# Rows for all 128 partitions: transfers with a repeated source and a matmul with ones in place of GpSimd's partition_broadcast

## The chip, the core and the metric

The kernel runs on one core of one Trainium2 chip. A core has a matrix engine (TensorE, PE in the profile, with its weight loads shown apart as PEld), a vector engine (VectorE, DVE), a scalar engine (ScalarE, ACT), GpSimd (POOL), and SyncE (SP), which here issues nearly all transfers between HBM and the on-chip memory. Each engine works through its own queue in the order that was fixed when the program was built, and waits where an operand isn't there yet. The metric is the device time of one execution in microseconds (us). PE's granted clock is given as a share of 2.4 GHz: 1.00 is 2.4 GHz, 0.50 is 1.2 GHz.

## What is computed

One decoder layer on x of 512 tokens by 1024 features, in float32. Three blocks follow one another, each with a normalization ahead (a gain row of 1024 numbers) and one behind (another gain row), so there are six gain rows in all:

```python
h = rms_norm(x, ffn1_pre_g)
x = x + 0.5 * rms_norm(swiglu(h, ffn1_w_gate, ffn1_w_up, ffn1_w_down), ffn1_post_g)
h = rms_norm(x, mix_pre_g)
proj = h @ w_in
...
mixed = jnp.concatenate([attn, ssm], axis=-1) @ w_out
x = x + rms_norm(mixed, mix_post_g)
h = rms_norm(x, ffn2_pre_g)
x = x + 0.5 * rms_norm(swiglu(h, ffn2_w_gate, ffn2_w_up, ffn2_w_down), ffn2_post_g)
```

`rms_norm(x, g)` is x times 1/sqrt(mean(x*x) + eps) times g, row by row. The mixer needs, beside matrices, three rows of 16 numbers (dt_bias, a_log, d_skip) and one number lambda, which is an exponential of two dot products.

## The kernel before

**Tiles.** Tokens lie on the 128 partitions, so x is four tiles t = 0 to 3 of 128x1024, and a gain row that multiplies a tile must stand in every partition: a tile of 128x1024 floats, 512 KB. `bcast` (L128 to L134) makes one: a 4 KB transfer into a tile `row` of one partition, and then `partition_broadcast` on GpSimd into the tile `t`. The three rows of 16 and lambda are put into one row of 49 numbers and go the same way, at L118, into `prm`. Both take their tiles from pools with few buffers (`ka` has 3).

**Normalization ahead of a block.** `prenorm_T` (L150) handles one tile. ACT squares and sums it (L147), POOL turns the sum into 1/sqrt(...) in two small operations (`rstd`, L140 and L141, tile `r`), DVE multiplies the tile by `r` and by the gain (L156, tile `kb`), PE transposes the result in eight pieces of 128x128 (L160), and ACT and DVE evacuate that in a high and a low part (L163), because every product is made of three passes over such split operands (`mm3`, L194 to L196).

**Start.** The program loads x tile 0, the gain `ffn1_pre_g`, x tile 1, and then the weights of the first four products of the FFN (two gate and two up blocks of 128 columns, `lead` in `ffn`, four 512 KB transfers named `raw`). Each weight is split on ACT (L175, `whi`) and on DVE (L177, `wlo`). Tiles 0 and 1 are normalized first, and the four lead products run on the token columns 0 to 255 (lines L228 and L194 to L196). x tiles 2 and 3 are loaded behind the lead weights, are normalized by `rest1`, with their transposes set into the last lead product, and then the lead products run on the columns 256 to 511. Further gain rows are fetched by `gain(...)`: for the first block while the lead products run. The rest of an FFN is a long stretch of products.

**Middle.** The mixer runs attention (`attention`, with lines L554 to L598), projections, and the chunked scan (`ssd`), woven into each other by fixed ratios. At the head of a chunk of the scan, `decay` has POOL make two 128x1024 products of a mask and a column (L641, tiles `kb` from `u` and `ah`, then from `u` and `al`), PE multiplies them (L653), and ACT takes the exponential (L654).

**Second FFN.** Built as the first: `rest2` (L913) normalizes tiles 2 and 3 while the lead products run on the first half.

**Order.** The build schedules the queues by a simulation of the engines, so a row in the code does not tell its place in a queue. On POOL the build puts a row named ISA ahead of each `partition_broadcast`, and another ahead of the next ordinary operation; in the trace these show as MODIFY_POOL_CONFIG, and are called a switch here. The broadcast itself is also printed as ISA.

Of the kernel before, what the change touches and what calls it, by code (L numbers as in the profile page):

```python
# [17 lines left out]
P = 128  # L18
D = 1024
# [10 lines left out]
class Layer:  # L30
# [48 lines left out]
    def mixer_consts(s, conv_w, conv_b, dt_bias, a_log, d_skip, subln, norm_g, lq1, lk1, lq2, lk2):  # L79
        nc = s.nc  # L80
        s.ones = s.t([P, P], F32, "ones")
        nc.gpsimd.memset(s.ones, 1.0)
        s.u1 = s.t([P, P], F32, "u1")
        nc.gpsimd.affine_select(s.u1, s.ones, pattern=[[-1, P]], base=-1, channel_multiplier=1,
                                compare_op=ALU.is_ge, fill=0.0)
        s.u2 = s.t([P, P], F32, "u2")
        nc.gpsimd.affine_select(s.u2, s.ones, pattern=[[1, P]], base=0, channel_multiplier=-1,
                                compare_op=ALU.is_ge, fill=0.0)

        rows = s.m((P, P))  # L90
        nr = 61 + 8
        nc.sync.dma_start(rows[0:48, :], conv_w.rearrange("k (t p) -> (k t) p", p=P))
        nc.sync.dma_start(rows[48:60, :], conv_b.rearrange("o (t p) -> (o t) p", p=P))
        nc.sync.dma_start(rows[60:61, 0:64], subln)
        nc.sync.dma_start(rows[60:61, 64:128], subln)
        nc.sync.dma_start(rows[61:69, :], norm_g.rearrange("o (t p) -> (o t) p", p=P))
        ps = s.pb()
        nc.tensor.transpose(ps[:, :nr], rows[:nr, :], s.ident[:nr, :nr])
        s.cols = s.t([P, nr], F32, "cols")
        nc.vector.tensor_scalar_mul(s.cols, ps[:, :nr], 0.5)  # L100
        nc.vector.tensor_scalar_mul(s.cols[:, 60:61], ps[:, 60:61], 1.0 - LAMBDA_INIT)

        row = s.m((1, 48 + 128))
        nc.sync.dma_start(row[:, 0:16], dt_bias)
        nc.sync.dma_start(row[:, 16:32], a_log)
        nc.sync.dma_start(row[:, 32:48], d_skip)
        for i, l in enumerate((lq1, lq2, lk1, lk2)):
            nc.sync.dma_start(row[:, 48 + 32 * i:80 + 32 * i], l)
        lam = s.t([1, 4], F32, "lam")
        nc.vector.tensor_mul(row[:, 48:112], row[:, 48:112], row[:, 112:176])  # L110
        nc.vector.tensor_reduce(lam[:, 0:2], row[:, 48:112].rearrange("p (a b) -> p a b", a=2),
                                axis=AX.X, op=ALU.add)
        nc.scalar.activation(lam[:, 0:2], lam[:, 0:2], AF.Exp)
        nc.scalar.activation(row[:, 16:32], row[:, 16:32], AF.Exp)
        nc.vector.tensor_scalar(row[:, 48:49], lam[:, 1:2], lam[:, 0:1], -LAMBDA_INIT,
                                op0=ALU.subtract, op1=ALU.add)
        s.prm = s.t([P, 49], F32, "prm")
        nc.gpsimd.partition_broadcast(s.prm, row[:, 0:49])  # L118
        s.nlam = s.prm[:, 48:49]

        s.qscale = s.t([P, 4], F32, "qscale")
        s.nslope = s.t([P, 48], F32, "nslope")[:, :16]
        for h in range(8):
            lo = (h % 2) * 64
            nc.gpsimd.memset(s.qscale[lo:lo + 64, h // 2:h // 2 + 1], 32.0 ** -0.5 * 2.0 ** (h + 1))
            nc.gpsimd.memset(s.nslope[:, 2 * h:2 * h + 2], -2.0 ** -(h + 1))

    def bcast(s, ap):  # L128
        nc = s.nc
        row = s.k4([1, D])  # L130
        nc.sync.dma_start(row, ap)
        t = s.k4([P, D])
        nc.gpsimd.partition_broadcast(t, row)
        return t  # L134


# [822 lines left out]
```

## Time and profile before

| what | us |
|---|---|
| median of 3 runs (1141.47 to 1144.44) | 1143.95 |
| the profiled execution, its own time | 1141.0 |
| its span, from the first to the last instruction | 1138.9 |
| mean granted PE clock in it | 0.981 |

The profile is of one execution. A time given for an instruction or a wait is from that execution, counted from the start of its span. In the timeline a row gives start, duration, engine, line, operation, tiles written and read, and in brackets how long the engine was idle before it and what ended that. "issue" there means that the engine waited for nothing that the profile can see. The table of windows gives busy time of each engine in a stretch, the granted PE clock, the mean share of the 16 DMA engines and what they moved.

### The profile page before, as it was taken

The page shows a single profiled execution, that of the slowest core. Times are in us where ns is not written, and L with a number is a line of the kernel's source. Part 1 is how long each engine was busy: PE and PEld are TensorE (multiplying, and loading weights), DVE is VectorE, ACT ScalarE, POOL GpSimd, SP SyncE. Part 2 cuts the span into 40 slices and gives each one's busy share as a digit, 9 for nine tenths or more (in the row PEclk, how much of TensorE's full clock was granted, in tenths as well). Part 3 has the DMA queues.
Part 4 walks back from the last instruction along what each step waited for, and adds up shares of the span by engine and source line. Part 5 has one row for each costly group of instructions (what it writes and reads, how often), then busy time and mean ns, then how long its engine had stood idle before and what let it go on. Part 6 is the DMA issues. An engine that isn't in the chain of part 4 may idle for free. (4 is left out here: it accounts for less than half of the span.)

```text
span 1138.9 us, 13158 instructions
## 1 busy us (share of the span) xinstructions
PE 1072.2 (94%) x5129; PEld 893.3 (78%) x5129; DVE 547.6 (48%) x861; ACT 396.9 (35%) x673; POOL 89.5 (8%) x123
## 2 busy tenths in 40 slices
PE   2699999999999999999997989986999999999997
PEld 2688888888888887888875777876888888888885
DVE  2333433434333663686875987663234343353334
ACT  3242121322322453465652445443322212132231
POOL 3100000000000210000113351020000000000001
PEclk9899999999999999999998999997999999999999
DMA  5143241433323244543321103231333224143311
GB/s 166 56 128 94 70 133 56 130 93 107 97 93 95 93 126 138 156 128 104 93 75 38 56 19 110 76 111 56 106 98 93 93 73 131 56 130 97 106 38 74
DMA packets 135444, 107.94 MB, mean 95 GB/s; under 512 B 5772, under 2 KB 116432, under 8 KB 135382
## 3 DMA queue, kind: packets, MB, share of 16 engines
q1 hardware_dynamic: 134806, 105.00, 30.7%
q0 software_dynamic: 576, 2.10, 0.5%
q8 instruction: 40, 0.66, 0.2%
q14 instruction: 22, 0.18, 0.0%
HBM read 96.60 MB, written 4.19 MB: 88 GB/s over the span
## 5 line engine op out<-in xcount | busy, mean ns | idle before, releaser
L175 ACT CAST whi<-raw 128x1024 fp32r<-128x1024 f32 x176 | 183.2, 1051 | 496.0 <-PE pa L195 210.9
L195 PE MATMUL pa<-blk,whi 128*128 128x512 f32 (+1 forms) x864 | 332.4, 385 | 0.0
L196 PE MATMUL pa<-blk,wlo 128*128 128x512 f32 (+1 forms) x864 | 331.0, 385 | 0.0
L177 DVE TENSOR_TENSOR wlo<-raw,whi 128x1024 fp32r<-128x1024 f32 x176 | 217.6, 1244 | 230.8 <-ACT whi L175 225.1
L194 PE MATMUL pa<-blk,whi 128*128 128x512 f32 (+1 forms) x736 | 279.3, 380 | 0.0
L196 PEld LDWEIGHTS pa<-blk,wlo 128*128 128x128 f32 x864 | 163.3, 189 | 32.7 <-issue 1.2
L195 PEld LDWEIGHTS pa<-blk,whi 128*128 128x128 f32 x864 | 163.4, 189 | 31.7 <-issue 0.7
L194 PEld LDWEIGHTS pa<-blk,whi 128*128 128x128 f32 x736 | 138.3, 188 | 26.3
L258 DVE TENSOR_TENSOR at<-cv,pa 128x512 f32<-128x512 f32 x42 | 28.9, 687 | 130.4 <-PE pa L196 130.4
L195 PE MATMUL pa<-wlo,blk 128*128 128x512 f32 x216 | 85.3, 396 | 0.0
L196 PE MATMUL pa<-whi,blk 128*128 128x512 f32 x216 | 84.8, 396 | 0.0
L140 POOL TENSOR_SCALAR r<-ss 128x1 f32<-128x1 f32 x32 | 12.9, 405 | 805.7 <-DVE ss L332 728.9
L283 PE MATMUL pb<-whi,blk 128*128 128x512 f32 x224 | 65.1, 389 | 0.0
L192 PE MATMUL pa<-blk,whi 128*128 128x512 f32 x128 | 52.8, 412 | 0.0
L283 PEld LDWEIGHTS pb<-whi,blk 128*128 128x128 f32 x224 | 41.9, 188 | 8.6
L194 PE MATMUL pa<-whi,blk 128*128 128x512 f32 x120 | 47.3, 394 | 0.0
L196 PEld LDWEIGHTS pa<-whi,blk 128*128 128x128 f32 x216 | 40.3, 188 | 8.6 <-issue 0.5
L195 PEld LDWEIGHTS pa<-wlo,blk 128*128 128x128 f32 x216 | 40.7, 188 | 8.1 <-issue 0.7
L290 DVE TENSOR_TENSOR blk<-blk,pb 128x512 f32<-128x512 f32 x24 | 15.4, 683 | 64.3 <-PE pb L283 64.3
L160 PE MATMUL pt<-ident,kb 128*128 128x128 f32 x72 | 11.7, 309 | 32.6 <-DVE kb L156 31.5
L283 PE MATMUL po<-whi,blk 128*128 128x512 f32 x112 | 41.3, 389 | 0.0
L283 PE MATMUL pa<-whi,blk 128*128 128x512 f32 x112 | 41.3, 389 | 0.0
(207 smaller groups left out, 1394.6 us busy)
## 6 DMA issues: line engine op xcount, KB each, us to landing
raw<-in_ffn_w_gate_dram SPq DMA_DIRECT2D x44, 512.0 KB
raw<-in_ffn_w_up_dram SPq DMA_DIRECT2D x44, 512.0 KB
raw<-in_ffn_w_down_dram SPq DMA_DIRECT2D x44, 512.0 KB
raw<-in_w_in_dram SPq DMA_DIRECT2D x32, 512.0 KB
blk<-kc SPq DMA_DIRECT2D x96, 64.0 KB
raw<-in_w_out_dram SPq DMA_DIRECT2D x12, 512.0 KB
blk<-in_x_dram SPq DMA_DIRECT2D x4, 512.0 KB
x_d<-blk POOLq DMA_DIRECT2D x4, 512.0 KB, 3.5
```

What stands on the lines that cost most here:

```text
L140: nc.gpsimd.tensor_scalar(r, ss, mul / n, eps, op0=ALU.mult, op1=ALU.add)
L160: ins = nc.tensor.transpose(ps[:, i * P:(i + 1) * P], hx[:, (4 * b + i) * P:(4 * b + i + 1) * P], s.ident)
L175: s.nc.scalar.copy(hi, raw)
L177: s.nc.vector.tensor_sub(lo, raw, hi)
L192: mm(ps, a[0], b[0], start=first, stop=False)
L194: mm(ps, a[0], b[0], start=first, stop=False)
L195: mm(ps, a[0], b[1], start=False, stop=False)
L196: return mm(ps, a[1], b[0], start=False, stop=last).ins
L258: nc.vector.tensor_mul(pr, sg, pu)
L283: nc.tensor.matmul(pd[c], a[:, ts], w[:, c * S:(c + 1) * S], start=st, stop=sp)
L290: nc.vector.tensor_add(a, a, pd[c])
```

## The change

`bcast` no longer has a row tile and a GpSimd operation: one transfer fills all 128 partitions, with the same 4 KB of HBM as the source of each. `prm` is made by a matmul of a row of 128 ones with the row of 49, into a PSUM buffer of the tag `pb`, and a copy on DVE.

```diff
         s.prm = s.t([P, 49], F32, "prm")
-        nc.gpsimd.partition_broadcast(s.prm, row[:, 0:49])
+        ps = s.pb()
+        nc.tensor.matmul(ps[:, 0:49], s.ones[0:1, :], row[:, 0:49], start=True, stop=True)
+        nc.vector.tensor_copy(s.prm, ps[:, 0:49])
         s.nlam = s.prm[:, 48:49]
...
     def bcast(s, ap):
         nc = s.nc
-        row = s.k4([1, D])
-        nc.sync.dma_start(row, ap)
         t = s.k4([P, D])
-        nc.gpsimd.partition_broadcast(t, row)
+        nc.sync.dma_start(t, ap.broadcast_to([P, D]))
         return t
```

The queues follow. SP issues the transfers of the start; `blk` are the x tiles, `ka` the gain tiles, `raw` the weights. Before:

```order
L768 DMA blk_70<-in_x_dram 128x1024
L131 DMA ka_73<-in_ffn_pre_g_dram 1x1024
L768 DMA blk_70<-in_x_dram 128x1024
L185 DMA raw_131<-in_ffn_w_gate_dram 128x8x128
L185 DMA raw_162<-in_ffn_w_up_dram 128x8x128
L185 DMA raw_195<-in_ffn_w_gate_dram 128x8x128
L185 DMA raw_226<-in_ffn_w_up_dram 128x8x128
L131 DMA ka_2264<-in_ffn_post_g_dram 1x1024
L768 DMA blk_71<-in_x_dram 128x1024 x2
L272 DMA raw_410<-in_ffn_w_down_dram 128x1024
L131 DMA ka_2268<-in_mix_pre_g_dram 1x1024
```

And with the change:

```order
L768 DMA blk_70<-in_x_dram 128x1024
L133 DMA ka_73<-in_ffn_pre_g_dram 128x1024
L768 DMA blk_70<-in_x_dram 128x1024
L185 DMA raw_129<-in_ffn_w_gate_dram 128x8x128
L185 DMA raw_160<-in_ffn_w_up_dram 128x8x128
L185 DMA raw_193<-in_ffn_w_gate_dram 128x8x128
L185 DMA raw_224<-in_ffn_w_up_dram 128x8x128
L133 DMA ka_2262<-in_ffn_post_g_dram 128x1024
L133 DMA ka_2264<-in_mix_pre_g_dram 128x1024
L768 DMA blk_71<-in_x_dram 128x1024 x2
L272 DMA raw_408<-in_ffn_w_down_dram 128x1024
```

The gain transfers are 128 rows instead of one, and that of `mix_pre_g` now stands ahead of x tiles 2 and 3 instead of behind them.

On POOL, at the start, between the making of the identity matrix and the first two normalizations, before:

```order
masks.py:199 AFFINE_SELECT ident_63<-ident_63 128x128
L133 ISA
L133 ISA ka_75<-ka_73 128x1024
L140 ISA
L140 TENSOR_SCALAR r_85<-ss_83 128x1
L141 TENSOR_TENSOR r_85<-r_85,mhalf_68 128x1
```

And with the change:

```order
masks.py:199 AFFINE_SELECT ident_63<-ident_63 128x128
L140 TENSOR_SCALAR r_83<-ss_81 128x1
L141 TENSOR_TENSOR r_83<-r_83,mhalf_68 128x1
L140 TENSOR_SCALAR r_106<-ss_104 128x1
L141 TENSOR_TENSOR r_106<-r_106,mhalf_68 128x1
```

The broadcast and the two switches around it are gone from the queue; nothing takes their place.

On POOL, at the head of the scan's chunks in the middle, before:

```order
L641 TENSOR_TENSOR kb_4545<-u_424_2676,ah_3145 128x1024
L133 ISA
L133 ISA ka_5591<-ka_5589 128x1024
L641 ISA
L641 TENSOR_TENSOR kb_4547<-u_424_2676,al_3146 128x1024
L641 TENSOR_TENSOR kb_4563<-u_424_2676,ah_3145 128x1024
L133 ISA
L133 ISA ka_5595<-ka_5593 128x1024
L641 ISA
L641 TENSOR_TENSOR kb_4565<-u_424_2676,al_3146 128x1024
```

And with the change:

```order
L598 TENSOR_TENSOR ms_750_4200<-ms_750_4200,mhalf_68 128x8
L641 TENSOR_TENSOR kb_4541<-u_421_2670,ah_3141 128x1024
L641 TENSOR_TENSOR kb_4543<-u_421_2670,al_3142 128x1024
L641 TENSOR_TENSOR kb_4559<-u_421_2670,ah_3141 128x1024
L641 TENSOR_TENSOR kb_4561<-u_421_2670,al_3142 128x1024
L641 TENSOR_TENSOR kb_4677<-u_421_2670,ah_3141 128x1024
L598 TENSOR_TENSOR ms_806_4441<-ms_806_4441,mhalf_68 128x8
L641 TENSOR_TENSOR kb_4679<-u_421_2670,al_3142 128x1024
```

Two broadcasts with four switches stood between the two halves of a chunk's products; the halves now follow one another. The other places on POOL are alike: seven broadcasts and their 14 switches are gone. PE has one row more, the matmul for `prm`, and DVE one, its copy.

## Rows read from the trace of the kernel before

**Rows 1.** Page, section 1: busy us (share of the span) xinstructions

```profile
PE 1072.2 (94%) x5129; PEld 893.3 (78%) x5129; DVE 547.6 (48%) x861; ACT 396.9 (35%) x673; POOL 89.5 (8%) x123
```

**Rows 2.** Waits of PE: who waited for whom: us, times, longest

```profile
PE pt L160 <- DVE kb L156: 31.5, 2, 21.5
PE pb L160 <- DVE kb L156: 12.2, 1, 12.2
PE pb L653 <- POOL kb L641: 10.1, 2, 8.0
PE pb L696 <- DVE kc L678: 1.8, 1, 1.8
```

**Rows 3.** Timeline of POOL: the broadcasts and the operations behind them

```profile
10.52 1.30 POOL L133 PARTITION_BROADCAST ka<-ka  x1 [8.89 <-issue]
19.79 0.18 POOL L140 TENSOR_SCALAR r<-ss 128x1 f32<-128x1 f32 x1 [7.97 <-issue]
42.62 0.18 POOL L140 TENSOR_SCALAR r<-ss 128x1 f32<-128x1 f32 x1 [8.24 <-issue]
588.17 1.89 POOL L641 TENSOR_TENSOR kb<-u,al 128x1024 fp32r<-128x1024 f32 x1 [7.02 <-issue]
607.83 1.89 POOL L641 TENSOR_TENSOR kb<-u,al 128x1024 fp32r<-128x1024 f32 x1 [7.39 <-issue]
776.32 0.18 POOL L140 TENSOR_SCALAR r<-ss 128x1 f32<-128x1 f32 x1 [7.65 <-issue]
```

**Rows 4.** Windows: length; busy us of PE, PEld, DVE, ACT, POOL; PE clock; DMA; GB/s

```profile
2.00:15.00 13.00, 0.00 (x0) 0.00 (x0) 0.00 (x0) 3.41 (x6) 1.30 (x1) 1.00 0.97 317
44.90:48.40 3.50, 3.45 (x17) 3.48 (x18) 2.58 (x3) 1.18 (x2) 0.55 (x1) 0.50 0.02 5
560.00:580.00 20.00, 20.00 (x102) 16.87 (x102) 19.27 (x45) 10.98 (x28) 3.73 (x3) 1.00 0.27 70
588.00:620.00 32.00, 21.87 (x93) 17.97 (x94) 16.34 (x22) 9.23 (x15) 10.52 (x6) 0.79 0.10 34
591.00:594.50 3.50, 3.50 (x10) 2.75 (x9) 1.89 (x3) 1.54 (x3) 1.90 (x1) 0.51 0.42 150
609.80:615.00 5.20, 5.20 (x12) 4.12 (x13) 2.61 (x4) 1.75 (x3) 3.55 (x2) 0.50 0.01 3
778.50:782.10 3.60, 3.54 (x17) 3.54 (x18) 2.58 (x5) 2.10 (x3) 0.00 (x0) 0.50 0.00 0
```

**Rows 5.** Timeline of ACT: start, first work on each of three transfers

```profile
4.37 1.06 ACT L147 ACTIVATE kb<-blk 128x1024 f32<-128x1024 f32 x1 [2.30 <-DMA blk<-in_x_dram]
6.71 1.06 ACT L147 ACTIVATE kb<-blk 128x1024 f32<-128x1024 f32 x1 [1.18 <-DMA blk<-in_x_dram]
8.54 1.04 ACT L175 CAST whi<-raw 128x1024 fp32r<-128x1024 f32 x1 [0.69 <-DMA raw<-in_ffn_w_gate_dram]
```

**Rows 6.** Timelines of the engines: a normalization, from sum to products

```profile
410.38 1.06 ACT L147 ACTIVATE kb<-blk 128x1024 f32<-128x1024 f32 x1 [4.28 <-DVE blk L336]
...
411.90 0.56 POOL L141 TENSOR_TENSOR r<-r,mhalf 128x1 f32<-128x1 f32 x1
...
22.55 1.41 DVE L156 SCALAR_TENSOR_TENSOR kb<-blk,r,ka 128x512 f32<-128x512 f32 x2 [0.45 <-POOL r L141]
...
25.14 1.25 PE L228 MATMUL pa<-blk,whi 128*128 128x256 f32 x8 [0.17 <-ACT blk L163]
...
44.95 1.94 PE L160 MATMUL pt<-ident,kb 128*128 128x128 f32 x8 [10.03 <-DVE kb L156]
```

**Rows 7.** Timelines of ACT and PE, second FFN, tiles 2 and 3

```profile
762.12 1.06 ACT L147 ACTIVATE kb<-blk 128x1024 f32<-128x1024 f32 x1 [3.34 <-DVE blk L336]
...
765.37 1.03 PE L160 MATMUL pt<-ident,kb 128*128 128x128 f32 x8
```

**Rows 8.** Timelines of PE and DVE: a small matmul, the row of 49

```profile
412.66 0.22 PE L98 MATMUL pb<-ident,m 69*128 69x69 f32 x1
...
416.81 0.20 DVE L115 TENSOR_SCALAR m<-lam 1x1 f32<-1x1 f32 x1 [0.27 <-ACT lam L113]
```

## The prediction

> **What bounds the kernel now.** I read the page first: PE is busy for 1072.2 of 1138.9 us [rows 1]. The kernel is bound by its products, and a change that touches none of them can win only PE's 67 idle us and what the clock takes. So the next view is the list of PE's waits [rows 2]. Three lines hold nearly all of it: PE waits for normalized tiles (`kb`, L156) for 31.5 us in two waits, 21.5 at the start of the program and 10.0 later, and for 12.2 us in one wait in the second FFN; and it waits for POOL's mask products (L641) for 10.1 us in two, 8.0 and 2.1. The fourth line, 1.8 us, is of another kind.
>
> DVE, named in the first two lines, is not the cause: it waits for `r`, which POOL makes. POOL's timeline tells the rest [rows 3]. The first broadcast starts at 10.52 after 8.89 us in which POOL did nothing and waited for nothing that the profile sees, and the operation behind it starts 8 us after its end (7.97 idle). The same holds at 42.62 (8.24), 588.17 (7.02), 607.83 (7.39) and 776.32 (7.65). So the broadcast itself, 1.30 us, is cheap; the switches on both sides of it are what costs, 8.89 + 7.97 = 16.9 us at the first place, and in each of the five cases it is the operation behind the second switch for which PE is waiting in the end.
>
> The last view is the table of windows, for the clock [rows 4]. After each long stall PE runs for a while at 0.50, the lower level of 1.2 GHz: 3.5 us from 44.9, 3.5 from 591.0, 5.2 from 609.8 and 3.6 from 778.5. Work done at half speed costs half of that time again: 1.75, 1.7, 2.6 and 1.8 us, 7.9 in all. A stall thus costs more than its length.
>
> **The start, and the second stall of the first FFN.** Without switches POOL is free for `r` as soon as the sum of squares is there. What is late next are the transfers, since a gain row is now 512 KB, as large as an x tile or a weight. ACT begins to work on the first, second and third 512 KB transfer at 4.37, 6.71 and 8.54 [rows 5], and the transfers of the start ran at 317 GB/s [rows 4], so 524,288 bytes take 1.65 us. In SP's new order the gain is second, x tile 1 third, x tiles 2 and 3 tenth and eleventh. Taking a repeated source to cost what an x tile costs (the nearest row: same tile, same queue, same number of rows), they arrive at 6.7, 8.5, 8.54 + 7 x 1.65 = 20.1 and 21.7.
>
> From the start of a tile's sum of squares to the end of `r` it takes 411.90 + 0.56 - 410.38 = 2.08 us where nothing is in the way [rows 6]. For tile 1: 8.54 + 2.08 = 10.6. From L156 on that tile to the first dense product the trace has 25.14 - 22.55 = 2.6 us [rows 6]; the products begin at 13.2, where they began at 25.14. Between the transposes of tiles 0 and 1, PE is idle for nearly 2 us.
>
> The dense stretch ran until 44.95 - 10.03 = 34.9, 9.8 us [rows 6]; it now ends at 23.0. Then PE needs tile 2: 20.1 + 2.08 + 1.41 for L156 [rows 6] = 23.6, and tile 3: 21.7 + 2.08 + 1.41 = 25.2. The transposes of tile 2, at 44.95 before, start at 23.6: 21.35 us earlier. The slow stretch behind the old stall (1.75) goes too, since 0.6 us of waiting is left in place of 10. I take off 0.5 for tile 3, which comes 1.6 us after tile 2 while the transposes between take 1.0 [rows 7]. **Together 22.6 us.**
>
> The lead weights come 1.65 us later than before. That is hidden: their splits for leads 1 to 3 stand behind the evacuation of tile 1 in any case, and end some 12 us earlier. If the cover were gone, it would cost 1.65.
>
> Here the price of a repeated source decides, and the trace of before has none. From below I exclude a gain against an x tile, because as many bytes must be written. From above: if one DMA engine did all of it, at 317/16 = 20 GB/s, a gain tile would take 26.5 us. Both ends are kept for the cases below. On the side of the dear end stands a rule of the Trainium skill, "DMA: Bandwidth & Descriptors", section "Latency and other measured facts": copies whose partitions read at a row pitch of 4 MiB ran at 103 GB/s where a pitch of 512 KiB gave 207, by an unverified inference because streams in lockstep meet on one HBM channel. A pitch of zero is not among its cases; taken over as a factor of two, it would make this term smaller by about 6.6 us and the sum below 43.1 instead of 49.7. No row of this case shows it.
>
> **The middle.** Without the switches the second half of a chunk's mask products needs only its buffer. For chunk 0 PE would have it before it asks; for chunk 1 the buffer comes free with the last attention transposes, which stand ahead of the place in PE's queue. So 10.1 us of waiting go [rows 2], and 1.7 + 2.6 us of slow clock behind them [rows 4]: 14.4. What is late next is DVE. From 588 to 620 it is busy for 16.34 of 32 us [rows 4]; with 14.4 us gone that is 16.3 of 17.6, or 93%. It ran like this before: from 560 to 580 it was busy for 19.27 of 20 us while PE was busy for 20.00 [rows 4]. I take off 1.0 for what DVE brings late. **13.4 us.** The three gain transfers here stand where the row loads stood in SP's queue and wait, as those did, for a `ka` buffer that attention leaves; behind them are weights with four buffers. The DMA engines are busy to 0.27 and 0.10 in these windows [rows 4], so 3 x 1.65 us are hidden. Without that cover they would cost 5.
>
> **The second FFN.** The last broadcast, at 767, goes. Tile 3's sum starts at 762.12 [rows 7], so `r` is there at 764.2 and L156 ends at 765.6. PE comes to these transposes at 765.37 + 1.03 = 766.4 [rows 7] and finds them ready: 12.2 us of waiting [rows 2] and 1.8 of clock. **14.0 us.**
>
> **The small row.** The matmul for `prm` goes into PE's queue. The nearest operation is a float32 transpose of 0.22 us [rows 8]; with its weight load I count 0.3. The row of 49 is ready at 417.0 [rows 8], and the matmul's place lies behind the transposes of the last tile and seven products, after that. The `prm` copy on DVE is used much later. **Minus 0.3.**
>
> **Sum:** 22.6 + 13.4 + 14.0 - 0.3 = 49.7 us. Against the profiled execution's 1141.0 that is 1091.3. The median of the runs is 3 us above that execution, so I forecast **1092**.
>
> **The rivals.**
> - *A repeated source at half the rate.* 128 reads of the same 4 KB could get in each other's way. Three gain tiles stand ahead of x tile 3, each 1.65 us dearer: 4.9 us later, and a stall of some 5 us before tile 2, behind which PE would run slow again (1.75). 1092 + 6.6 = 1098.6. Against it: each of 16 engines has its own rows to write. For it: no row shows otherwise.
> - *DVE takes over in the middle.* DVE's steps there hang on ACT, which hangs on PE, and the idle time in the 588 to 620 window gave it room. If half of the 14.4 us come back as PE waiting for DVE, 1092 + 6.2 = 1098.
> - *The other side: the transfer uses one engine.* A zero step could keep the source from being spread. Then 26.5 us each, and everything behind it in that engine's queue waits: x tile 3 at 21.7 + 3 x 24.85 = 96, its transposes at about 99.8 in place of 25.2. That loses 74.6 against the forecast: 1092 + 74.6 = 1167, slower by 23. It decides from 49.7/3 = 16.6 us more per tile, 18.2 us each, or 29 GB/s. Against it: the tile has 128 rows, as an x tile has, and that is spread.
> - *The change doesn't do what it says.* If POOL still switched for some other reason, the time would stay near 1143. The queue built for the change has no row for it behind the making of the identity matrix.
>
> A further risk is small: PE's idle 2 us between tiles 0 and 1 could bring the slow clock, as the stall of 2.1 us did [rows 2, 4]. That costs 1.75, of which 0.6 lies under the wait for tile 2.
>
> **How the numbers follow.** The forecast case has 0.74, half rate 0.13, DVE 0.06, one engine 0.03, no effect 0.02; 0.02 are left for what I don't see. The likeliest case alone reaches from 1088 (no loss to DVE or tile 3, and the lower run-to-run level) to 1097 (slow clock at the start, a transfer a third dearer). The range of 1087 to 1103 takes in the two rivals at 1098 with 4 us beyond them, and leaves out the last two. A measurement of this kernel can tell about 0.3%, 3.4 us, from no change. Faster 0.95, the same 0.02, slower 0.03.
>
> **What would show it.** In the new profile PE's three waits should be gone from the top of the list: first dense products (L228) near 13, transposes of tile 2 near 24, no wait for L641 over 1 us, no wait at the second FFN's tile 3, and the clock at 1.00 in the stretches around 45, 592, 612 and 780 of before. POOL should show no MODIFY_POOL_CONFIG for L133 or L140. ACT's first work on x tile 1 tells the price of a repeated source: near 8.5 if I am right, 10.2 at half rate. The forecast is wrong if x tile 3 arrives well past 22, or if DVE becomes the releaser of PE's waits between 575 and 610.

## The result, and the profile after

The changed kernel takes 1091.59 us (median of 4 runs, 1089.36 to 1091.88), the kernel before beside it 1144.2 (4 runs, 1141.47 to 1146.07): a ratio of 0.9538, interval 0.9515 to 0.9561. The forecast was 1092, range 1087 to 1103. The profiled execution took 1091.88, its span is 1090.1 and its mean PE clock 0.996.

First the page, the line that answers to [rows 1]:

```profile
PE 1068.3 (98%) x5131; PEld 889.8 (82%) x5131; DVE 548.3 (50%) x862; ACT 397.7 (36%) x673; POOL 81.3 (7%) x116
```

PE's busy time is 3.9 us less, its products being the same; its idle time fell from 67 to 22 us. POOL has 7 instructions fewer, the seven broadcasts. PE's waits, to be set beside [rows 2]:

```profile
PE pt L160 <- DVE kb L156: 7.7, 1, 7.7
PE pb L696 <- DVE kc L678: 1.8, 1, 1.8
PE pb L160 <- DVE kb L156: 1.3, 1, 1.3
```

The waits of 10.0, 12.2, 8.0 and 2.1 are gone, and the first one fell from 21.5 to 7.7. On POOL's timeline the operations of [rows 3] now look like this (the bracket holds the idle time and what ended it):

```profile
6.00 0.19 POOL L140 TENSOR_SCALAR r<-ss 128x1 f32<-128x1 f32 x1 [4.63 <-ACT kb L147]
...
570.30 1.90 POOL L641 TENSOR_TENSOR kb<-u,al 128x1024 fp32r<-128x1024 f32 x1 [0.58 <-issue]
...
728.52 0.19 POOL L140 TENSOR_SCALAR r<-ss 128x1 f32<-128x1 f32 x1 [2.08 <-ACT kb L147]
```

Each `r` is released by ACT's sum of squares. The 7 to 8 us without a visible reason, ahead of the same lines before, have no counterpart, and the trace has no MODIFY_POOL_CONFIG for L133 or L140. The clock, in the stretches that answer to the four slow ones of [rows 4], and in one that is new (length; busy us of PE, PEld, DVE, ACT, POOL; PE clock; DMA; GB/s):

```profile
2.00:15.00 13.00, 5.99 (x26) 5.37 (x27) 6.84 (x11) 6.96 (x12) 5.85 (x25) 1.00 0.99 339
24.20:27.70 3.50, 3.50 (x33) 3.50 (x32) 1.92 (x4) 2.32 (x5) 0.00 (x0) 1.00 0.00 0
565.50:583.10 17.60, 17.60 (x95) 14.95 (x94) 14.63 (x20) 9.46 (x15) 8.23 (x4) 1.00 0.29 90
638.00:641.00 3.00, 3.00 (x6) 1.69 (x6) 2.81 (x6) 1.21 (x3) 0.00 (x0) 0.50 0.00 0
730.50:734.10 3.60, 3.60 (x34) 3.60 (x33) 2.48 (x5) 2.91 (x5) 0.00 (x0) 1.00 0.00 0
```

The four are at 1.00 (565.5 to 583.1 is what was 588 to 620, and holds two of them). The fourth line is a slow stretch behind the wait at L696, which stood in the trace of before too, at the same length but without a fall of the clock. More on it below.

Where the time went is read by laying the same products of the two traces side by side: by how much a product comes earlier than before is what was won up to there. Five products of before (PE's timeline):

```profile
385.04 0.39 PE L194 MATMUL pa<-whi,blk 128*128 128x512 f32 x1
...
426.00 0.39 PE L195 MATMUL pa<-blk,whi 128*128 128x512 f32 x1
...
627.40 0.39 PE L195 MATMUL pa<-blk,whi 128*128 128x512 f32 x1
...
709.99 0.39 PE L195 MATMUL pa<-wlo,blk 128*128 128x512 f32 x1
...
1116.78 0.39 PE L194 MATMUL pa<-whi,blk 128*128 128x512 f32 x1
```

The same five of the changed kernel:

```profile
362.30 0.39 PE L194 MATMUL pa<-whi,blk 128*128 128x512 f32 x1
...
403.84 0.39 PE L195 MATMUL pa<-blk,whi 128*128 128x512 f32 x1
...
590.80 0.39 PE L195 MATMUL pa<-blk,whi 128*128 128x512 f32 x1
...
675.07 0.39 PE L195 MATMUL pa<-wlo,blk 128*128 128x512 f32 x1
...
1067.89 0.39 PE L194 MATMUL pa<-whi,blk 128*128 128x512 f32 x1
```

| up to | earlier by | this stage | forecast |
|---|---|---|---|
| first FFN's products | 22.74 | +22.7 | +22.6 |
| behind the `prm` matmul | 22.16 | −0.6 | −0.3 |
| behind the two chunks in the middle | 36.60 | +14.4 | +13.4 |
| behind the wait at L696 | 34.92 | −1.7 | not foreseen |
| last products | 48.89 | +14.0 | +14.0 |

The sum, 48.9, stands against a forecast of 49.7. It compares two single executions: that of before is at the low end of its runs, that of the changed kernel at the high end. By the medians the gain is 52.6.

### The profile page after: what moved, and what is told of

It reads as the page before. It is cut to its first block, busy times and chain, and to the rows that moved or that the text cites. A ratio compares the mean times of both kernels' runs of the same rounds, so it can differ in the third digit from the quotient of the medians.

```text
span 1090.1 us, 13117 instructions
## 1 busy us (share of the span) xinstructions
PE 1068.3 (98%) x5131; PEld 889.8 (82%) x5131; DVE 548.3 (50%) x862; ACT 397.7 (36%) x673; POOL 81.3 (7%) x116
## 5 line engine op out<-in xcount | busy, mean ns | idle before, releaser
L196 PE MATMUL pa<-whi,blk 128*128 128x512 f32 x216 | 85.0, 397 | 0.0
L140 POOL TENSOR_SCALAR r<-ss 128x1 f32<-128x1 f32 x32 | 12.1, 379 | 802.9 <-DVE ss L332 735.8
L283 PE MATMUL pb<-whi,blk 128*128 128x512 f32 x224 | 65.1, 389 | 0.0
L283 PEld LDWEIGHTS pb<-whi,blk 128*128 128x128 f32 x224 | 41.9, 188 | 8.6
L194 PE MATMUL pa<-whi,blk 128*128 128x512 f32 x120 | 47.5, 395 | 0.0
L283 PE MATMUL pa<-whi,blk 128*128 128x512 f32 x112 | 41.3, 389 | 0.0
L283 PE MATMUL po<-whi,blk 128*128 128x512 f32 x112 | 41.3, 389 | 0.0
L192 PE MATMUL pa<-whi,blk 128*128 128x512 f32 x96 | 39.6, 414 | 0.2 <-ACT blk L621 0.2
```

The costliest lines, as they stand in the source:

```text
L140: nc.gpsimd.tensor_scalar(r, ss, mul / n, eps, op0=ALU.mult, op1=ALU.add)
L192: mm(ps, a[0], b[0], start=first, stop=False)
L194: mm(ps, a[0], b[0], start=first, stop=False)
L196: return mm(ps, a[1], b[0], start=False, stop=last).ins
L283: nc.tensor.matmul(pd[c], a[:, ts], w[:, c * S:(c + 1) * S], start=st, stop=sp)
```

## The experiments

**Undoing the change at one group of gains at a time.** Theory: the gain of the change is the sum of four places. Each of four kernels makes one group of gain tiles by the old way and leaves the rest as changed:

```diff
-    def bcast(s, ap):
+    def bcast(s, ap, pool=False):
         nc = s.nc
+        if pool:
+            row = s.k4([1, D])
+            nc.sync.dma_start(row, ap)
+            t = s.k4([P, D])
+            nc.gpsimd.partition_broadcast(t, row)
+            return t
         t = s.k4([P, D])
...
-        g = s.bcast(ffn1_pre_g)
+        g = s.bcast(ffn1_pre_g, True)
```

That is keep_A; in B, C and D the flag is set in `gain` for one key: `post1` (the first FFN's post gain and the mixer's pre gain), `post` (the mixer's post gain and the second FFN's pre gain), `post2` (the last gain).

keep_A: 

> The changed kernel with the first gain row (ffn1_pre_g) still made by GpSimd's broadcast. Theory (the switches around a broadcast hold r, one place at a time, and the places add up): the first dense products begin near 25 again, tile 2's transposes near 35 with no stall there, since tiles 2 and 3 are long normalized; 10.7 us above the changed kernel, about 1102. Rival (the start's win comes from transfers or from the matmul for prm, not from this broadcast): no more than 2 us above it, 1092 to 1094.

keep_B: 

> The changed kernel with ffn1_post_g and mix_pre_g made by GpSimd's broadcast. Theory: dense products begin near 13, POOL gives r of tile 2 near 30, PE waits some 8 us before tile 2's transposes and then runs slow for 3.5 us; 10 us above the changed kernel, about 1102. With the 10.7 of the kernel that keeps the first row this gives the 22 us of the two places together. Rival (the two places hide one another, so that undoing one alone costs little): under 3 us above.

keep_C: 

> The changed kernel with mix_post_g and ffn2_pre_g made by GpSimd's broadcast. Theory: both stalls of PE for the mask products (2.1 and 8.0 us) come back with the slow clock behind them; 14.4 us above the changed kernel, about 1106. Rival (DVE bounds the middle anyway, and part of the win was already lost to it): 7 us above or less.

keep_D: 

> The changed kernel with the second ffn_post_g row made by GpSimd's broadcast. Theory: the wait of 12.2 us before tile 3's transposes in the second FFN and 1.8 us of slow clock come back; 14.0 us above the changed kernel, about 1105.6. Rival (this stall was covered by another wait that has gone too): under 7 us.

| kernel | median (4 runs) | ratio to before, interval | above the changed kernel |
|---|---|---|---|
| keep_A | 1104.09 | 0.9667, 0.9643 to 0.9691 | 12.5 |
| keep_B | 1102.04 | 0.9645, 0.9628 to 0.9662 | 10.4 |
| keep_C | 1106.03 | 0.9683, 0.9663 to 0.9704 | 14.4 |
| keep_D | 1104.67 | 0.9663, 0.9640 to 0.9685 | 13.1 |

The four add up to 50.4 us; all four undone at once, which is the kernel before but for `prm`, cost 52.6 by the medians. So the places add up, within the spread of the runs (1.6 to 5.3 us for one of the four), and none hides another. B, C and D cost about what was expected (10, 14.4 and 14.0). A was expected to cost 10.7: its first products begin at 27.97 in place of the expected 25, since POOL is idle for 11.0 us behind the broadcast, where it was 7.97 before [rows 3]; why is not shown. Each wait came back where it was, though not always with its old length (in C 14.0 us in place of 10.1). PE's waits in keep_B, keep_C and keep_D (line numbers behind `bcast` are higher by 6 in these kernels: L166 is L160 of the changed kernel, L659 is L653):

```profile
PE pt L166 <- DVE kb L162: 18.0, 2, 10.4
```

```profile
PE pb L659 <- POOL kb L647: 14.0, 2, 11.9
```

```profile
PE pb L166 <- DVE kb L162: 12.6, 2, 11.3
```

And the slow clock came back with them, as in keep_B behind the 10.4 us (the columns as above):

```profile
32.60:36.20 3.60, 3.57 (x17) 3.60 (x18) 2.58 (x3) 1.49 (x3) 0.56 (x1) 0.50 0.02 5
```

**Is it the broadcast or the switch?** A broadcast of 8 columns that nobody reads is put ahead of tile 3's `r` in the second FFN of the changed kernel:

```diff
         def rest2():
...
+            if t == 3:
+                nc.gpsimd.partition_broadcast(s.t([P, 8], F32, "dummy"), xt(x2, 3)[0:1, 0:8])
```

> The changed kernel with one GpSimd broadcast of 8 columns, whose result nobody reads, put ahead of r of tile 3 in the second FFN. Theory (the switches cost, not the broadcast's own work nor its transfer): it costs as much as the whole gain row there, 13 us, about 1104.5, with both idle times of 6 to 8 us on POOL around it. Rival (the cost goes with the size of the broadcast or with waiting for its data): under 3 us.

It took 1104.47 us (1101.7 to 1104.93), 0.9659 of before (0.9638 to 0.9681): 12.9 above the changed kernel, where the whole broadcast of keep_D had cost 13.1. POOL's timeline, and PE's row behind it:

```profile
729.29 0.28 POOL L906 PARTITION_BROADCAST dummy<-blk  x1 [5.67 <-issue]
736.32 0.18 POOL L140 TENSOR_SCALAR r<-ss 128x1 f32<-128x1 f32 x1 [6.75 <-issue]
```

```profile
738.55 1.97 PE L160 MATMUL pb<-ident,kb 128*128 128x128 f32 x8 [9.83 <-DVE kb L156]
```

The broadcast itself is down from 1.30 to 0.28 us and the loss is the same. What costs is the idle time on either side of it, 5.67 and 6.75 us: the switch there and the switch back. The rows of MODIFY_POOL_CONFIG stand at the start of each idle time, at 723.6 and 729.5; what POOL does in it, the trace doesn't tell.

**Does the repeated source cost anything?** The gain tiles are filled from 128 different rows of x instead, so that this kernel leaves the gains out:

```diff
-        nc.sync.dma_start(t, ap.broadcast_to([P, D]))
+        nc.sync.dma_start(t, s.x_d[0:P, :])
```

> The changed kernel with each gain tile filled by a transfer of the first 128 rows of x, 128 different rows of 4 KB, in place of one row repeated 128 times; the gains are thus left out and rows of x multiplied in their place. Theory (a repeated source costs what different rows cost): ACT's first work on x tile 1 at 7.9 and on tile 2 at 17.8, as in the changed kernel, within 0.5 us; time within 1 us of 1091.6. Rival (a repeated source is slower, or faster, than different rows): tile 2 arrives earlier, or later, by over 1 us.

1091.48 us (1091.01 to 1091.65), 0.9549 of before (0.9528 to 0.957): the same as the changed kernel. ACT's first work on x tiles 1 and 2, with the repeated source and then with different rows:

```profile
7.92 1.06 ACT L147 ACTIVATE kb<-blk 128x1024 f32<-128x1024 f32 x1 [2.01 <-DMA blk<-in_x_dram]
...
17.83 1.06 ACT L147 ACTIVATE kb<-blk 128x1024 f32<-128x1024 f32 x1 [1.41 <-DMA blk<-in_x_dram]
```

```profile
7.46 1.06 ACT L147 ACTIVATE kb<-blk 128x1024 f32<-128x1024 f32 x1 [1.39 <-DMA blk<-in_x_dram]
...
17.30 1.06 ACT L147 ACTIVATE kb<-blk 128x1024 f32<-128x1024 f32 x1 [0.88 <-DMA blk<-in_x_dram]
```

Tile 1, behind one gain, and tile 2, behind three, are each about 0.5 us later with the repeated source; it does not grow with the number of gain tiles, so it is no halved rate, which would have shown 1.65 us at tile 1 and 4.9 at tile 2. The rule of the Trainium skill that the forecast named ("DMA: Bandwidth & Descriptors", section "Latency and other measured facts": half the rate at a row pitch of 4 MiB) has no case of a pitch of zero. For that pitch this run shows no halving.

**Was the matmul for `prm` worth it?** `prm` goes back to GpSimd, the gains stay:

```diff
-        ps = s.pb()
-        nc.tensor.matmul(ps[:, 0:49], s.ones[0:1, :], row[:, 0:49], start=True, stop=True)
-        nc.vector.tensor_copy(s.prm, ps[:, 0:49])
+        nc.gpsimd.partition_broadcast(s.prm, row[:, 0:49])
```

> The changed kernel with the row of 49 (prm) still made by GpSimd's broadcast, the six gain rows by transfers. Theory: nothing waits for POOL there before 70 us later, so the two switches are hidden, and the 0.6 us that the matmul for prm takes out of PE's stretch come back: 1091.0, no difference that can be told from the changed kernel's 1091.6. Rival (these switches hold something too): slower by some us.

1089.85 us (1089.45 to 1090.29), 0.9537 of before (0.9519 to 0.9554): no difference that can be told. Nobody waited for that broadcast, although it switches like the others. In the changed kernel the matmul is this row of PE's; its copy takes DVE 0.21 us:

```profile
396.97 0.42 PE L119 MATMUL pb<-m,ones 1*128 1x49 f32 x2
```

The float32 matmul runs as two instructions. With the gaps around them PE's next products are 0.6 us later.

**The start: why it gained what was forecast, from other terms.** PE at the start of the changed kernel:

```profile
7.67 1.97 PE L160 MATMUL pt<-ident,kb 128*128 128x128 f32 x8 [7.67 <-DVE kb L156]
10.98 1.97 PE L160 MATMUL pb<-ident,kb 128*128 128x128 f32 x8 [1.34 <-DVE kb L156]
12.77 2.08 PE L228 MATMUL pa<-blk,whi 128*128 128x256 f32 x8
14.65 1.91 PE L228 MATMUL pa<-blk,wlo 128*128 128x256 f32 x8
...
24.22 1.03 PE L160 MATMUL pt<-ident,kb 128*128 128x128 f32 x8
```

The transposes last 1.97 us for eight, like those at 44.95 of before at a clock of 0.50 [rows 4, 6], and the first sixteen products 2.08 and 1.91 for eight, where eight took 1.25 before [rows 6]. The window from 2 to 15, above, says 1.00 all the while, but that is no reading: the first entry of the trace's record of the granted clock, at 1.00, begins at 16.51 us, and the table takes the stretch ahead of it as 1.00. The kernel before starts at the slow pace too (its first entry is at 24.47): its first transposes take 1.97 and 1.62 us for eight, with no gap between the two tiles, and its products run at 1.25 from the start. Behind the slow products PE reaches tile 2's transposes with no wait: tile 2 was there first. Two kernels tell whether the slow pace hangs on PE's own idleness. In `warm`, 40 transposes of the identity into an unread buffer run on PE before its first work, and 14 between the two tiles:

```diff
+        warm = s.po()
+        for i in range(40):
+            nc.tensor.transpose(warm[:, 0:P], s.ident, s.ident)
...
+            if t == 0:
+                with tc.issue_after(ins):
+                    for i in range(14):
+                        nc.tensor.transpose(warm[:, 0:P], s.ident, s.ident)
```

> The changed kernel with 40 transposes of the identity matrix on PE ahead of tile 0's transposes and 14 between those of tiles 0 and 1, into a buffer that the lead products later use. Theory (the first dense products of the changed kernel, 8 in 2.08 us where before they were 8 in 1.25, run at the lower clock, though the granted clock reads 1.00 there): they take 1.2 to 1.3 us again, tile 2's transposes start near 22.5 in place of 24.2, and the time falls by 1.7 us to 1090. Rival (they wait for their operands): they take as long as in the changed kernel, and the time stays at 1091.6.

In `x1_first`, `load_x(1)` is put ahead of `g = s.bcast(ffn1_pre_g)`:

> The changed kernel with x tile 1's transfer put ahead of the first gain's. Theory: at the start the path to the first products runs through the arrival of x tile 1 (ACT takes it up at 7.92 us in the changed kernel, and DVE's second tile, PE's transposes and the first product at 12.77 follow), so that with tile 1 second in the queue ACT takes it up near 6.3, and the first product starts earlier by as much as DVE allows; DVE must still wait for the gain, which now lands third, near 7.9, for both tiles: its first multiply starts near 7.9 in place of 6.6, its two tiles take 2 x 1.42 us, so tile 1 is done near 10.8 where it was near 11.3. Gain at the start 0.3 to 0.8 us, 1090.8 to 1091.3. Rival: the transposes of tile 2 near 24.2 are set by PE, whose first products run at half pace for as long as they do; a start that is 0.5 us earlier then gives nothing, 1091.6, within the spread of the runs.

`warm` took 1089.24 us (1088.46 to 1090.0), 0.9531 of before (0.9512 to 0.955), `x1_first` 1089.07 (1088.52 to 1089.95), 0.9529 (0.9516 to 0.9542). By the ratios neither is told apart from the changed kernel; the profiles show what each did (the record of the clock begins at 6.01 us in `warm` and at 12.01 in `x1_first`). `warm`, PE's timeline:

```profile
8.06 1.04 PE L160 MATMUL pt<-ident,kb 128*128 128x128 f32 x8
...
12.06 1.41 PE L228 MATMUL pa<-blk,whi 128*128 128x256 f32 x8
...
13.30 1.12 PE L228 MATMUL pa<-blk,wlo 128*128 128x256 f32 x8
...
23.30 1.04 PE L160 MATMUL pt<-ident,kb 128*128 128x128 f32 x8
```

`x1_first`, the same:

```profile
8.91 1.97 PE L160 MATMUL pt<-ident,kb 128*128 128x128 f32 x8 [8.91 <-DVE kb L156]
10.67 1.70 PE L160 MATMUL pb<-ident,kb 128*128 128x128 f32 x8
12.41 1.38 PE L228 MATMUL pa<-blk,whi 128*128 128x256 f32 x8
13.62 1.12 PE L228 MATMUL pa<-blk,wlo 128*128 128x256 f32 x8
...
23.11 1.04 PE L160 MATMUL pt<-ident,kb 128*128 128x128 f32 x8
```

In both, PE has no gap between the two tiles, and the products run at 1.12 for eight a few us sooner. Tile 2's transposes come 0.9 and 1.1 us earlier, but that is not the whole gain, since in these two kernels six more products stand ahead of them in PE's queue. The first product of L283, farther on in the first FFN, tells it. The rows give shortest, median and longest duration in ns, and then the first and the last start, in the changed kernel, `warm` and `x1_first`:

```profile
L283 PE MATMUL pb<-whi,blk x224: 389/389/398, 39.3 to 947.8; 128*128 128x512 f32 x112
```

```profile
L283 PE MATMUL pb<-whi,blk x224: 389/389/398, 37.6 to 944.4; 128*128 128x512 f32 x112
```

```profile
L283 PE MATMUL pb<-whi,blk x224: 389/389/398, 37.4 to 945.9; 128*128 128x512 f32 x112
```

It starts 1.7 and 1.9 us earlier. So the 1.7 expected of `warm` is there, though not the 22.5 for tile 2's transposes. For `x1_first` the expectation held only in its smaller part: tile 1's earlier arrival makes the first product 0.36 us earlier (12.41). Tile 0's transposes come 1.24 later, since DVE now begins at 8.11, with `r` there at 6.76: what is left for it to wait for is the gain, which lands third. The larger part comes from PE's idle 1.34 us between the tiles, which is gone, and with it most of the slow products. The rival held that the slow products would stay, and that was wrong.

**The wait at L696, and a version with all of it.** `best` joins `prm_pool` and `warm`; `best_x1` adds the order of `x1_first`; `fill` adds to that 14 transposes on PE inside the wait at L696 (L694 and L697 in these kernels):

```diff
                 pst = s.pb()
+                if g == 1 and c == 0:
+                    for i in range(14):
+                        nc.tensor.transpose(pst[:, 0:P], bn, s.ident)
                 ins = nc.tensor.matmul(pst, bn, xx[:, 1, :], start=True, stop=True)
```

best: 

> The changed kernel with prm kept on GpSimd and with 40 + 14 extra transposes of the identity on PE before the first ones of x and between the two tiles. Theory: the two effects add, as they lie in different places: 0.6 us of PE for the matmul in two passes that is gone, and 0.9 us at the start (1.7 more in those executions in which the slow clock after PE's 1.8 us wait at line 696 stays away): 1089.2 less 0.6 to 0.9, so 1088.3 to 1088.7. Rival: the broadcast of prm now delays something on GpSimd in this order, or the two single gains were spread of the runs: 1089.2 to 1091.6.

best_x1: 

> As the run before (prm on GpSimd, extra transposes), with x tile 1's transfer ahead of the first gain's. Theory: with PE's products at full pace from the start, nothing but the arrival of tile 1 and DVE stands ahead of the first product, so here the earlier tile 1 gives its 0.3 to 0.8 us even if it gives nothing in the changed kernel alone: 1087.7 to 1088.3. Rival: the tile that sets the end of the start is tile 2, whose transposes come at 23.3 behind the lead products and whose transfer is at the same place in the queue; nothing is gained, 1088.5.

fill: 

> As the run best_x1, with 14 extra transposes on PE inside the one wait of 1.83 us that is left in the middle (ahead of the matmul by which the scan's state is made, second half of the heads, first chunk). Theory: that wait is what brings the slow clock to the products behind it in many executions (0.50 for 3 us, 1.7 us lost, in the changed kernel, in distinct, and in part in x1_first and best_x1); with PE busy through it, the clock stays at 1.00 there in this profile, the matmul itself starts no later (DVE's late product sets it, not PE), and the median comes down from 1088.3 by up to 1.7, to 1086.6 to 1088.0. Rival: the wait has nothing to do with it (in best and warm it was there and the clock stayed at 1.00); then the low clock shows up behind it just as before, and the time is 1088.3 or, as the transposes run ahead of other work, up to 1 more.

| kernel | median | lowest, highest | ratio to before, interval |
|---|---|---|---|
| best | 1089.77 (4 runs) | 1087.53, 1090.56 | 0.9534, 0.9520 to 0.9548 |
| best_x1 | 1088.30 (4 runs) | 1087.46, 1089.08 | 0.9524, 0.9511 to 0.9537 |
| fill | 1087.33 (5 runs) | 1087.30, 1087.59 | 0.9521, 0.9506 to 0.9535 |

`best` did not come out below `warm` in its median and lies in the range of its rival; the sum of the single gains is not shown by it. `best_x1` lies at the upper edge of what was expected, but not by the reason given: its first product starts at 12.63, that of `best` at 12.09. `fill` behaved as expected. The windows around that wait in `best_x1`, then in `fill`:

```profile
632.00:635.00 3.00, 1.19 (x9) 0.77 (x8) 3.00 (x3) 0.48 (x2) 2.07 (x1) 1.00 0.00 0
635.00:638.00 3.00, 2.98 (x6) 1.90 (x7) 3.00 (x6) 1.21 (x3) 0.12 (x1) 0.60 0.00 0
```

```profile
632.00:635.00 3.00, 3.00 (x25) 2.57 (x24) 3.00 (x2) 0.60 (x2) 2.07 (x1) 1.00 0.00 0
635.00:638.00 3.00, 2.93 (x13) 1.99 (x12) 3.00 (x7) 0.73 (x2) 0.59 (x2) 1.00 0.02 5
```

With PE busy from 632 to 635 the clock stays at 1.00 behind it, and the five runs of `fill` lie within 0.3 us, where the four of `best_x1` are spread over 1.6 and those of `best` over 3.0. The wait alone doesn't decide it. Two profiles have the same wait, that of the changed kernel and that of `warm`, with a different pace of the matmul behind it:

```profile
637.67 2.04 PE L696 MATMUL pb<-kc,bn 128*128 128x512 f32 x2 [1.83 <-DVE kc L678]
```

```profile
636.00 1.12 PE L696 MATMUL pb<-kc,bn 128*128 128x512 f32 x2 [1.83 <-DVE kc L678]
```

Of the 13 profiles with this wait, seven have the slow stretch behind it and six have not. The spread goes with the clock: in the changed kernel, `warm`, `x1_first`, `best` and `best_x1` every run with a mean granted clock of 0.996 or less is 0.8 us or more above every run of the same kernel with 0.997 or more, and all five of `fill` are at 0.998 or 0.999. That the clock falls at this place is seen only in the profiled executions, so the likeliest reading, not a shown one, is that in some executions the wait brings the slow clock and in others not. What decides between the two stays open. The start adds to the spread: in six kernels whose start is the same as far as tile 2 (the changed kernel among them), the record of the clock begins anywhere from 13.92 to 17.03 us, and tile 2's transposes start from 23.09 to 24.38.

`fill` is the best version that was run: 4.3 us below the changed kernel by the medians, but 1.9 by the ratios (0.9521 against 0.9538), whose intervals overlap, as the two were run beside different runs of the kernel before.

## Why the prediction was right

**The bound and its cause** were read rightly. PE waited for `r`, and `r` for POOL's switches. dummy_D shows the switches as the whole price in the second FFN, and the four undone groups add up to the gain (50.4 of 52.6).

**The number was hit in part by luck.** The sum of 49.7 came off the profiled execution, 1141.0, and gave 1091.3; the step from there to 1092 was not worked out from the 3 us by which the median lay above that execution. Off the median of before, 1143.95, the same sum gives 1094.3. The measured gain is 52.6 by the medians and 48.9 in the profiles, so the sum lies between the two.

**Start and second stall: right sum, two terms off.** The forecast said first products at 13.2, tile 2's transposes at 23.6 after a wait of 0.6, and 0.5 lost to tile 3. The products began at 12.77 and tile 2's transposes at 24.22 without any wait, though x tiles 2 and 3 were taken up at 17.83 and 19.07 in place of 20.1 and 21.7. The step "524,288 bytes take 1.65 us" took the rate of the start before, 317 GB/s from 2 to 15. In the changed kernel the seven transfers from x tile 1 to x tile 2 took 17.83 − 7.92 = 9.91 us, 1.42 each. So the transfers were not what was late, and nothing was lost to tile 3. The other way went the pace of PE's first products: the dense stretch, "9.8 us", became 24.22 − 12.77 = 11.45, 1.65 more. Most of it is the slow pace: the first sixteen products took about 1.5 us longer than in `x1_first` (2.08 and 1.91 against 1.38 and 1.12). That is the "further risk" of a slow clock between tiles 0 and 1, which the forecast named with 1.75 and called small. It came about a little differently: PE was slow from its first transposes on, and the gap kept it slow. It did not show in the total because three terms of the transfers had been too dear: 0.4 for the first products, 0.6 of waiting and 0.5 for tile 3. That the two errors cancel is chance.

**The price of a repeated source** was taken as an x tile's. `distinct` puts it at 0.5 us more at tile 1 and no more at tile 2. Both rivals on it, half rate and one engine, fall.

**The middle: 14.4 in place of 13.4.** The 1.0 taken off for DVE was not needed. DVE was busy for 14.63 of the 17.60 us that the two chunks now take, against a forecast of 16.3, and PE for all of them. The rival by which DVE takes over falls.

**The second FFN: 14.0, as forecast.** Tile 3's transposes follow those of tile 2 without a wait at 1.00.

**The small row:** −0.6 in place of −0.3; the one matmul is two instructions on PE.

**What was missing:** the 1.7 us behind the wait at L696. The forecast called that wait "of another kind" and left it, since the trace of before showed no slow clock behind it. That a wait of 1.83 us had passed without a price in one execution was no proof that it has none.

## What to carry to other kernels

On an engine that must be switched for one kind of operation, price the operation by the idle time ahead of it and ahead of the next ordinary one (12 to 18 us in the kernel before and in dummy_D, for 0.3 to 1.3 us of work), and ask who waits for the next one: where somebody does, a transfer that fills all partitions from one row is cheap, and where nobody does, as for `prm`, the switch costs nothing that could be told here. When a large stall goes, look at what the waiting engine does in the first microseconds of the new schedule: its pace there may be set by its own idleness, not by its inputs. Cheap filler work on PE inside a short wait can keep the clock up behind it: here the runs then lay within 0.3 us in place of 1.6, and the median was 1.0 lower, with ratio intervals that overlap.

## What the runs showed of the hardware

- A granted clock of 1.00 at the program's start is no measurement. Eight products took 2.08 us in a window that reads 1.00, and 1.12 later at the same reading; the record of the clock has no entry ahead of 16.51 us in the changed kernel, 12.01 in `x1_first` and 6.01 in `warm`, and at these times the pace rises.
- DVE's late product, the cause of the wait at L696, is by these rows a collision. This multiplication, with both inputs in SBUF, takes 0.68 us in the other chunks, and 2.38 where it starts within POOL's mask product. DVE's rows and POOL's, of the changed kernel:

```profile
600.79 0.68 DVE L678 TENSOR_TENSOR kc<-kc,dec 128x512 f32<-128x512 f32 x1
...
635.23 2.38 DVE L678 TENSOR_TENSOR kc<-kc,dec 128x512 f32<-128x512 f32 x1
```

```profile
634.99 2.08 POOL L641 TENSOR_TENSOR kb<-u,al 128x1024 fp32r<-128x1024 f32 x1 [0.86 <-PE po L673]
```

  POOL's ends at 637.07 and DVE's 0.54 us later, about the 0.68 that it takes alone. The Trainium skill, "SBUF — State Buffer", section "Who interferes with whom", says that a DVE instruction with two inputs in SBUF contends with a GpSimd instruction that reads SBUF, and calls the contention an exclusive lock; these rows agree, with 1.70 us lost. L667, whose first input is in PSUM, takes its usual 0.68 us also where it starts (611.43) within a mask product (611.29 to 613.26). Moving one of the two was not tried.
- A transfer of 512 KB with one 4 KB row as the source of all partitions costs what 128 different rows cost, within 0.5 us.
